# Two of eight column-block pairs of each SwiGLU input product in seven block products, with single plain columns between their half steps

## The chip, the core and the metric

One core of a Trainium2 chip runs the whole program. The metric is the device time of one execution in microseconds, the median of three runs. TensorE (PE in the profile) multiplies and writes to eight PSUM banks of 128 x 512 float32; VectorE (DVE) and ScalarE (ACT) empty the banks and prepare operands; SyncE (SP) issues the DMAs of the weights.

## The reference

Two layers on 256 tokens of width 2048. Each layer has three sublayers, each followed by a residual and a layer norm:

```python
x = layer_norm(ALPHA * x + 0.5 * swiglu(x, *ffn1[i]), *ln1[i])
x = layer_norm(ALPHA * x + mixers[i](x), *ln2[i])
x = layer_norm(ALPHA * x + 0.5 * swiglu(x, *ffn2[i]), *ln3[i])

def swiglu(x, w_in, w_out):
    a, gate = jnp.split(x @ w_in, 2, axis=-1)
    return (jax.nn.silu(a) * gate) @ w_out
```

The four `w_in` are 2048 x 8192 and the four `w_out` 4096 x 2048, all float32. The mixers are stick-breaking attention (layer 0) and causal window pooling (layer 1). The change touches only how `x @ w_in` and `silu(a) * gate` are computed, in all four SwiGLUs.

## The kernel before, in words

Activations lie with the features on the partitions and the 256 tokens beside them. Every float32 operand is split into two float32r parts, hi and lo, and a product is the sum of hi*hi, lo*hi and hi*lo. The tiles `xs` hold the parts of x, sixteen tiles of 128 features.

A weight block of 512 columns comes in chunks of 512 rows (1 MB, one DMA into `raw`, three buffers). `chunk` makes the parts of each chunk in two halves: ACT writes `whi` (L133), DVE subtracts it from `raw` and writes `wlo` (L134), with five buffers of each. `gemm` then multiplies: for each 128 x 128 piece of weights as the stationary operand, one product of 512 columns with the hi and lo parts of x side by side (L157) and one of 256 columns with the lo weights (L160). Four banks `ps` collect four tiles of 128 features, and the last chunk finishes one tile after the other, so that `total` (L194 on ACT, L195 on DVE) empties a bank while the others are still written.

`ffn_in` runs eight pairs of column blocks, one of `a` and one of the gate. Where a layer norm comes just before, the first pairs are multiplied with x that is not yet normed (`ahead`, L151 to L153, three products of 258 columns instead of 512 + 256), and the norm's result is applied to `xq` and `xs` in the hooks of the last of them (`apply`, L266 and after). One pair goes that way in most sublayers, two in the second SwiGLU of layer 0 (`npairs=2`). The gated tiles `g` are split into parts and multiplied with `w_out` in `sublayer_end`; the last sublayer does that with tokens as the stationary operand and 512 weight columns moving (L572 to L574), as `values` of the attention does (L428 to L430).

The Tile scheduler sets the order of each engine's instructions when the program is built; on the chip each engine goes through its list in order and waits on semaphores.

Of the kernel before, what the change touches and what calls it, by code (L numbers as in the profile page):

```python
# [13 lines left out]
P = 128  # L14
# [8 lines left out]
WINDOWS = (2, 4, 8, 16)  # L23
ALPHA = 4 ** 0.25
# [11 lines left out]
def trunk(ctx: ExitStack, tc: tile.TileContext, a: dict, out: bass.AP):  # L36
# [4 lines left out]
    whis = ctx.enter_context(tc.tile_pool(name="whis", bufs=5))  # L41
    wlos = ctx.enter_context(tc.tile_pool(name="wlos", bufs=5))
# [24 lines left out]
    # The tensor engine runs at its full clock only after a while of work: products for  # L67
    # nothing, until the first data is here.
# [7 lines left out]
    # tri[k', k] = 1 where k' >= k; past[k, q] = 1 where k < q, twice.  # L76
# [20 lines left out]

    def split(dst, hi_src, lo_src):
# [18 lines left out]
    def chunk(w, r, c, fine=False, step=4):  # L117
        """Four 128-row tiles of 512 columns of w, in halves of hi and lo parts."""
# [87 lines left out]
    class Norm:  # L206
        """LN of what x holds, less a shift: its statistics, 1 / std and -mean on all partitions,
        and its result, for four tiles at a time. Ahead of it, xs = [hi | lo] of gain * x."""
# [12 lines left out]
        def add(self, t):  # L221
            """Tiles t and t + 1."""
# [5 lines left out]
            else:  # L228
                sq = tmp.tile([P, 2 * T], F32, tag="sq", name="sq")
# [3 lines left out]
            gx = tmp.tile([P, 2, T], F32, tag="gx", name="gx")  # L233
# [4 lines left out]
        def stats(self):  # L238
            # Sums over the features, by token: means, then mean squares.
# [31 lines left out]
    def sublayer_end(w, rhs, factor, gname, bname, hooks=None, one=0):  # L271
        """x <- LN(ALPHA x + factor y): LN of x + (factor / ALPHA) y, with eps / ALPHA**2."""
# [43 lines left out]
    def ffn_in(w_in, norm, hooks=None, npairs=1):  # L316
        gs = [None] * (FF // P)
        for grp in range(FF // 512):
            acts = []
            nm = norm if grp < npairs else None  # L320

            def evac_a(f, ps, acts=acts, nm=nm):
                s = tmp.tile([P, T], F32, tag=f"act{f}", bufs=1, name="act")
# [304 lines left out]
```

## Time and profile before

| | |
|---|---|
| three runs | 2683.4, 2683.8, 2683.8 us; median 2683.8 us |
| span of the profiled execution | 2681.8 us; the median run is 2.0 us longer |
| busy: PE, DVE, ACT | 2666.7 us (99%), 1675.7 us (62%), 1365.4 us (51%) |
| granted TensorE clock | 0.998 of full speed over the span |
| DMA | 499.61 MB, mean 186 GB/s |

PE is busy nearly without a gap. A matmul's busy time in the rows is longer than its slot, since one begins before the one ahead of it has ended; the slot is the distance of two starts. In the same way DVE's instructions overlap a little at their ends. Only instructions that the profile shows are counted as busy.

### The profile page before, as it was taken

The numbers are of one execution on the slowest core, as the hardware profiler recorded it, in microseconds if no ns is written. First come the engines' busy times: TensorE is split into PE (matmuls) and PEld (weight loads), VectorE is DVE, ScalarE is ACT, GpSimd is POOL, SyncE is SP. The second block draws the span as 40 slices with busy tenths as digits, with TensorE's granted clock in tenths as the row PEclk, the third lists the DMA queues.
The fourth block names the chain that finished last, engine by engine and source line by source line (L and its number), as shares of the span: only waits on it lengthen the run. The fifth ranks groups of instructions, "written<-read, shape, count | busy, mean of one in ns | idle before, by whom it ended". The sixth has DMA issues, their size and how long they took to land.

```text
span 2681.8 us, 38727 instructions
## 1 busy us (share of the span) xinstructions
PE 2666.7 (99%) x15916; PEld 2365.1 (88%) x15916; DVE 1675.7 (62%) x2298; ACT 1365.4 (51%) x1990; POOL 11.9 (0%) x28
## 2 busy tenths in 40 slices
PE   9999999999999999999999999999999999999998
PEld 8888888899999888888988888889888998888886
DVE  6555556585686555565765555667878775555545
ACT  5444444467565444444654444445555565444432
POOL 0000000000000000000000000000000000000000
PEclk9999999999999999999999999999999999999999
DMA  7555555554455555555555555554555545555653
GB/s 255 188 188 187 189 188 189 189 174 162 153 190 183 187 186 186 199 177 201 173 189 189 189 189 189 189 189 170 192 189 176 201 174 182 186 186 187 228 193 126
DMA packets 71521, 499.61 MB, mean 186 GB/s; under 512 B 7984, under 2 KB 8624, under 8 KB 12080
## 3 DMA queue, kind: packets, MB, share of 16 engines
q1 hardware_dynamic: 70704, 495.05, 52.4%
q8 instruction: 124, 2.03, 0.3%
q0 software_dynamic: 640, 2.10, 0.2%
q14 instruction: 53, 0.43, 0.0%
HBM read 495.02 MB, written 2.10 MB: 185 GB/s over the span
## 4 chain that ended last, share of the span: by engine, by line
PE 99%; DVE 1%; DMA 0%; SPq 0%; ACT 0%; issue 0%; DVEq 0%; ACTq 0%
PE ps L157 50%; PE ps L160 26%; PE ps L152 5%; PE ps L151 5%; PE ps L153 5%; PE y L573 2%; PE y L572 2%; PE y L574 2%; PE v L430 1%; PE v L428 1%; PE v L429 1%; DMA xq<-in_x 0%; PE cum L407 0%; DVE z L547 0%; PE bc L257 0%; PE st L244 0%
## 5 line engine op out<-in xcount | busy, mean ns | idle before, releaser
L134 DVE TENSOR_TENSOR wlo<-raw,whi 128x1024 fp32r<-128x1024 f32 (+1 forms) x946 | 1144.3, 1212 | 905.8 <-ACT whi L133 901.2
L133 ACT CAST whi<-raw 128x1024 fp32r<-128x1024 f32 (+1 forms) x946 | 982.0, 1041 | 1080.1 <-PE ps L157 851.9
L157 PE MATMUL ps<-xs,whi 128*128 128x512 f32 x3968 | 1389.8, 396 | 1.1 <-ACT whi L133 0.7
L160 PE MATMUL ps<-xs,wlo 128*128 128x256 f32 x3968 | 1100.5, 280 | 1.0 <-DVE wlo L134 1.0
L157 PEld LDWEIGHTS ps<-xs,whi 128*128 128x128 f32 x3968 | 744.8, 189 | 173.4 <-ACT whi L133 1.0
L160 PEld LDWEIGHTS ps<-xs,wlo 128*128 128x128 f32 x3968 | 748.3, 189 | 7.3 <-DVE wlo L134 1.5
L157 PE MATMUL ps<-g,whi 128*128 128x512 f32 x1536 | 534.9, 394 | 0.0
L160 PE MATMUL ps<-g,wlo 128*128 128x256 f32 x1536 | 427.8, 280 | 0.0
L157 PEld LDWEIGHTS ps<-g,whi 128*128 128x128 f32 x1536 | 287.2, 187 | 65.3
L160 PEld LDWEIGHTS ps<-g,wlo 128*128 128x128 f32 x1536 | 289.7, 189 | 1.1
L152 PE MATMUL ps<-xs,whi 128*128 128x258 f32 (+1 forms) x896 | 252.7, 284 | 0.0
L151 PE MATMUL ps<-xs,whi 128*128 128x258 f32 (+1 forms) x896 | 251.7, 283 | 0.0
L153 PE MATMUL ps<-xs,wlo 128*128 128x258 f32 (+1 forms) x896 | 245.5, 282 | 0.0
L152 PEld LDWEIGHTS ps<-xs,whi 128*128 128x128 f32 x896 | 169.6, 189 | 0.2
L151 PEld LDWEIGHTS ps<-xs,whi 128*128 128x128 f32 x896 | 168.9, 188 | 0.0
L153 PEld LDWEIGHTS ps<-xs,wlo 128*128 128x128 f32 x896 | 167.6, 190 | 0.0
L194 ACT COPY half<-ps 128x256 f32<-128x256 f32 x264 | 97.1, 369 | 121.0 <-PE ps L157 119.6
L572 PE MATMUL y<-wlo,g 128*128 128x512 f32 x256 | 99.6, 389 | 0.0
L573 PE MATMUL y<-whi,g 128*128 128x512 f32 x256 | 99.6, 389 | 0.0
L574 PE MATMUL y<-whi,g 128*128 128x512 f32 x256 | 99.4, 389 | 0.0
L157 PE MATMUL ps<-y,whi 128*128 128x512 f32 x256 | 89.6, 396 | 0.0
L195 DVE TENSOR_TENSOR act<-ps,half 128x256 f32<-128x256 f32 x124 | 52.1, 421 | 46.6 <-ACT half L194 46.6
(151 smaller groups left out, 1677.0 us busy)
## 6 DMA issues: line engine op xcount, KB each, us to landing
raw<-in_l_ffn_w_in SPq DMA_DIRECT2D x252, 1024.0 KB, 4.8
raw<-in_l_ffn_w_out SPq DMA_DIRECT2D x127, 1024.0 KB, 4.8
raw<-in_l_pool_w_in SPq DMA_DIRECT2D x32, 1024.0 KB, 4.9
raw<-in_l_sb_w_qkv SPq DMA_DIRECT2D x24, 1024.0 KB, 4.8
raw<-in_l_pool_w_out SPq DMA_DIRECT2D x16, 1024.0 KB, 4.9
raw<-in_l_sb_w_o SPq DMA_DIRECT2D x8, 1024.0 KB, 4.9
raw<-in_l_pool_w_grp SPq DMA_DIRECT2D x4, 1024.0 KB, 4.9
raw<-in_l_ffn_w_in SPq DMA_DIRECT2D x6, 512.0 KB, 9.4
```

Of the source, the lines that this page charges most:

```text
L133: nc.scalar.copy(hi[:, i], src)
L134: nc.vector.tensor_tensor(out=lo[:, i], in0=src, in1=hi[:, i].bitcast(F32), op=ALU.subtract)
L151: nc.tensor.matmul(ps[:, :one], hi[:, cs], x[:, 0, :one], start=first, stop=False)
L152: nc.tensor.matmul(ps[:, :one], hi[:, cs], x[:, 1, :one], start=False, stop=False)
L153: nc.tensor.matmul(ps[:, :one], lo[:, cs], x[:, 0, :one], start=False, stop=last)
L157: nc.tensor.matmul(ps.rearrange("p (h n) -> p h n", h=2), hi[:, cs], x, start=first, stop=last)
L160: nc.tensor.matmul(ps[:, :T], lo[:, cs], x[:, 0], start=False, stop=False)
L194: nc.scalar.copy(t, ps[:, T:])
L195: nc.vector.tensor_tensor(out=dst, in0=ps[:, :T], in1=t, op=ALU.add)
L572: nc.tensor.matmul(ps[m], gh, lo, start=kk == 0, stop=False)
L573: nc.tensor.matmul(ps[m], gl, hi, start=False, stop=False)
L574: nc.tensor.matmul(ps[m], gh, hi, start=False, stop=kk == nk - 1)
```

## The change

In each SwiGLU the eight column-block pairs are now made in three ways.

- The first pair goes through `gemm` or `ahead` as before (`npairs=2` is gone).
- The last two pairs (`SEVENS = 2`) go through `Seven.run`. It takes the 256 x 2048 by 2048 x 1024 product as a 2 x 2 block product (tokens, features and columns halved) and does seven block products of 128 tokens x 1024 features x 512 columns instead of eight. Eight steps of 128 features each load 1 MB with the four weight blocks; DVE forms four sums of them (`ta`, `tb`, L400); all seven operands are split into parts; seven banks p1 to p7 collect the products, three matmuls of 512 columns a step each (L422 to L424), with the tokens as the stationary operand. `prepare` makes the sums of x and their parts, sixteen instructions of 128 x 512 on DVE and eight on ACT in each SwiGLU. At the end DVE adds the seven banks up, and after the gating PE transposes the tiles (eight transposes a pair) back to features on the partitions.
- The five pairs between are cut into 40 units of 128 columns (`column`): one DMA of 1 MB, two halves of parts, 16 x (512 + 256) matmul columns into one bank, which ACT copies out. Four go ahead of the seven products, one after each half step of them, and three at the end.

The gated tiles are kept whole in float32 and split later (`settle`). There are six buffers of `whi` and `wlo` instead of five, and two of the sums. The diff, cut to its core:

```diff
+SEVENS = 2
...
-    whis = ctx.enter_context(tc.tile_pool(name="whis", bufs=5))
-    wlos = ctx.enter_context(tc.tile_pool(name="wlos", bufs=5))
+    sums = ctx.enter_context(tc.tile_pool(name="sums", bufs=2))
+    whis = ctx.enter_context(tc.tile_pool(name="whis", bufs=6))
+    wlos = ctx.enter_context(tc.tile_pool(name="wlos", bufs=6))
...
+    def column(w, t):
+
+        raw = raws.tile([P, KT, P], F32, tag="raw", name="raw")
+        nc.sync.dma_start(raw, w[t])
...
+        ps = bank("pc")
+        for k in range(KT):
...
+                nc.tensor.matmul(ps.rearrange("p (h n) -> p h n", h=2), his[k], whole[k], start=k == 0,
+                                 stop=k == KT - 1)
...
+                nc.tensor.matmul(ps[:, :T], los[k], whole[k][:, 0], start=False, stop=False)
...
+        c = wide("col")
+        nc.scalar.copy(c, ps)
+        return c
...
+        def prepare(self, q):
+
+            a11, a21 = (xq[q][:, :, m * P:(m + 1) * P] for m in range(2))
+            a12, a22 = (xq[q + 2][:, :, m * P:(m + 1) * P] for m in range(2))
+            t = [wide(f"s{i}").rearrange("p (j n) -> p j n", j=4) for i in range(4)]
+            for dst, x, y, op in ((t[0], a21, a22, ALU.add), (t[1], t[0], a11, ALU.subtract),
+                                  (t[3], a12, t[1], ALU.subtract), (t[2], a21, a11, ALU.subtract)):
+                nc.vector.tensor_tensor(out=dst, in0=x, in1=y, op=op)
+            for i in (0, 1, 3, 2):
+                hi, lo = (scratch(16 + 8 * q + 2 * i + h, F32R, f"s{i}{q}{h}").rearrange("p (j n) -> p j n", j=4)
+                          for h in range(2))
+                nc.scalar.copy(hi, t[i])
+                nc.vector.tensor_tensor(out=lo, in0=t[i], in1=hi.bitcast(F32), op=ALU.subtract)
+                for j in range(4):
+                    self.s[i, 4 * q + j] = hi[:, j], lo[:, j]
...
+        def run(self, w, grp, between):
...
+                raw = raws.tile([P, 4, 512], F32, tag="raw", name="raw")
+                nc.sync.dma_start(raw, w[grp, i])
+                b11, b2, b22, b21 = raw[:, 1], raw[:, 2:4], raw[:, 3], raw[:, 2]
...
+                ta, tb = (sums.tile([P, 2, 512], F32, tag="sum", name=n) for n in ("ta", "tb"))
...
+                parts(h11, l11, b11)
+                hb, lb = pair()
+                parts(hb, lb, b2)
+
+                for dst, x, y in ((ta, raw[:, 0:1].to_broadcast([P, 2, 512]), raw[:, 1:4:2]),
+                                  (tb[:, 0], b22, ta[:, 0]), (tb[:, 1], b21, tb[:, 0])):
+                    nc.vector.tensor_tensor(out=dst, in0=x, in1=y, op=ALU.subtract)
+                ha, la = pair()
+                parts(ha, la, ta)
+                ht, lt = pair()
+                parts(ht, lt, tb)
...
+                x1, x2 = xs[i], xs[i + 8]
+                products = {
+                    1: ((x1[:, 0, :P], x1[:, 1, :P]), h11, l11),
+                    2: ((x2[:, 0, :P], x2[:, 1, :P]), hb[:, 0], lb[:, 0]),
+                    3: (self.s[3, i], hb[:, 1], lb[:, 1]),
+                    5: (self.s[0, i], ha[:, 0], la[:, 0]),
+                    7: (self.s[2, i], ha[:, 1], la[:, 1]),
+                    6: (self.s[1, i], ht[:, 0], lt[:, 0]),
+                    4: ((x2[:, 0, P:T], x2[:, 1, P:T]), ht[:, 1], lt[:, 1]),
+                }
+                order = (1, 2, 6, 5, 3, 7, 4) if i == 7 else tuple(products)
+                for h in range(2):
+                    for n in (order[:4] if h == 0 else order[4:]):
+                        (xh, xl), hi, lo = products[n]
+                        if i == 0:
+                            ps[n - 1] = bank(f"p{n}")
+                        p = ps[n - 1]
+                        nc.tensor.matmul(p, xh, hi, start=i == 0, stop=False)
+                        nc.tensor.matmul(p, xl, hi, start=False, stop=False)
+                        nc.tensor.matmul(p, xh, lo, start=False, stop=i == 7)
+                    if (i, h) != (7, 1):
+                        between(i, h)
...
+            nc.scalar.copy(s1, p1)
+            add(c11, p2, s1)
+            add(u2, p6, s1)
+            add(u4, p5, u2)
+            add(c12, p3, u4)
+            add(c22, p7, u4)
+            add(u2, p7, u2)
+            add(c21, p4, u2)
...
+        seven.prepare(0)
+        seven.prepare(1)
+        todo = list(range(4, 4 * (ng - SEVENS)))
...
+        early = len(units) - 16 * SEVENS
+        for _ in range(early // 2):
+            unit()
+        if hooks:
+            hooks()
...
+        def between(i, h):
+            unit()
+            if lates and (i, h) == (0, 1):
+                lates.pop()()
...
+        for grp in range(ng - SEVENS, ng):
+            acts, gates = seven.run(w_seven, grp - ng + SEVENS, between)
+            unit()
+            lates.append(gated(grp, silu(acts, acts), gates))
+        settle(range(8))
+        unit()
+        settle(range(8, 16))
+        lates.pop()()
+        while units:
+            unit()
+        settle(range(16, 32))
...
-    norm = ffn('l0_', 2, 'ln3', norm, npairs=2)
+    norm = ffn('l0_', 2, 'ln3', norm)
```

How the change moves the instructions, at two places. The first is PE in the first SwiGLU. Before, in a plain block, the last chunk goes from bank `ps0` to bank `ps1`, all four banks having been taken at the block's start (`xs` are the parts of x, `whi` and `wlo` those of the weights):

```order
L160 MATMUL ps0_779<-xs3_83,wlo_906 128x256
L157 MATMUL ps0_779<-xs3_83,whi_905 128x512
L160 MATMUL ps0_779<-xs3_83,wlo_906 128x256
L157 MATMUL ps0_779<-xs3_83,whi_905 128x512
L160 MATMUL ps1_780<-xs3_83,wlo_902 128x256
L157 MATMUL ps1_780<-xs3_83,whi_901 128x512
L160 MATMUL ps1_780<-xs3_83,wlo_902 128x256
```

Now, in the middle of the first run of seven products, a unit ends in bank `pc_1188`, the three matmuls of p1 follow, and the next unit begins in `pc_1269`:

```order
L341 MATMUL pc_1188<-xs3_86,whi_1184 128x512
L345 MATMUL pc_1188<-xs3_86,wlo_1185 128x256
L341 MATMUL pc_1188<-xs3_86,whi_1184 128x512
L422 MATMUL p1_828<-whi_1366,xs1_84 128x512
L423 MATMUL p1_828<-whi_1366,xs1_84 128x512
L424 MATMUL p1_828<-wlo_1367,xs1_84 128x512
L341 MATMUL pc_1269<-xs0_83,whi_1261 128x512
L345 MATMUL pc_1269<-xs0_83,wlo_1262 128x256 x2
L341 MATMUL pc_1269<-xs0_83,whi_1261 128x512
```

Seven of the eight banks hold p1 to p7 there, and both `pc` tiles lie in the one that is left; between the two units PE has three matmuls of 512 columns.

The second place is DVE in the second SwiGLU of layer 0, where the layer norm has just been applied and the first pair ends. Before, DVE empties the banks of the first gate block (`gate`) and makes the lo parts of the next chunks:

```order
L134 TENSOR_TENSOR wlo_7533<-raw_7530,whi_7532 128x1024
L134 TENSOR_TENSOR wlo_7537<-raw_7530,whi_7536 128x1024
L134 TENSOR_TENSOR wlo_7595<-raw_7592,whi_7594 128x1024
L189 SCALAR_TENSOR_TENSOR gate_7459<-rb_7174,aux_7460,ps0_7268 128x256
L189 SCALAR_TENSOR_TENSOR gate_7480<-rb_7174,aux_7481,ps1_7269 128x256
L191 TENSOR_TENSOR gate_7459<-gate_7459,rb_7174 128x256
L191 TENSOR_TENSOR gate_7480<-gate_7480,rb_7174 128x256
L336 SCALAR_TENSOR_TENSOR gate_7459<-gate_7459,aux_7460,act_7198 128x256
L336 SCALAR_TENSOR_TENSOR gate_7480<-gate_7480,aux_7481,act_7216 128x256
L134 TENSOR_TENSOR wlo_7599<-raw_7592,whi_7598 128x1024
```

Now the sums for the seven products (`s0`, `s1`, ... by `prepare`, their lo parts as `s001`, `s011`, ...) and the first steps' operands stand among them, up to the parts of the unit after the first half step (`wlo_7864`):

```order
L198 TENSOR_TENSOR gate_7549<-gate_7549,rb_7193 128x256
L198 TENSOR_TENSOR gate_7567<-gate_7567,rb_7193 128x256
L367 TENSOR_TENSOR s1_7610<-s0_7609,xq1_80 128x512
L372 TENSOR_TENSOR s011_7618<-s0_7609,s010_7617 128x512
L506 SCALAR_TENSOR_TENSOR gw1_7548<-gate_7549,aux_7550,act_7252 128x256
L506 SCALAR_TENSOR_TENSOR gw1_7548<-gate_7567,aux_7568,act_7252 128x256
L325 TENSOR_TENSOR wlo_7842<-tb_7825,whi_7841 128x1024
L367 TENSOR_TENSOR s3_7612<-xq3_82,s1_7610 128x512
L367 TENSOR_TENSOR s2_7611<-xq1_80 128x512
L325 TENSOR_TENSOR wlo_7864<-raw_7861,whi_7863 128x1024
```

DVE's list has gained the sums of x, the sums of the weights and the larger number of parts in this stretch; the chunks of plain blocks that stood here are gone from it.

## Rows read from the trace of the kernel before

**Rows 1.** The page: the span, and part 1, busy us of each engine

```profile
span 2681.8 us, 38727 instructions
...
PE 2666.7 (99%) x15916; PEld 2365.1 (88%) x15916; DVE 1675.7 (62%) x2298; ACT 1365.4 (51%) x1990; POOL 11.9 (0%) x28
```

**Rows 2.** Waits of PE: us in total, times, longest us

```profile
PE idle L71 <- DVE one_t L73: 1.1, 1, 1.1
...
PE ps L157 <- DVE gate L195: 0.5, 1, 0.5
```

**Rows 3.** Timeline of PE, plain block: start us, us, operation, idle before

```profile
2399.82 0.28 PE L160 MATMUL ps<-xs,wlo 128*128 128x256 f32 x1
...
2405.45 0.28 PE L160 MATMUL ps<-xs,wlo 128*128 128x256 f32 x1
```

**Rows 4.** Timeline, `values`: 512 weight columns moving, tokens stationary

```profile
670.71 0.40 PE L428 MATMUL v<-wlo,xs 128*128 128x512 f32 x1
...
673.50 0.39 PE L428 MATMUL v<-wlo,xs 128*128 128x512 f32 x1
```

**Rows 5.** Timeline of PE, `w_out` of the last sublayer, same form

```profile
2519.72 0.39 PE L573 MATMUL y<-whi,g 128*128 128x512 f32 x1
...
2523.80 0.39 PE L573 MATMUL y<-whi,g 128*128 128x512 f32 x1
```

**Rows 6.** Timeline of PE, `ahead`: three products of 258 columns

```profile
1292.31 0.29 PE L152 MATMUL ps<-xs,whi 128*128 128x258 f32 x1
...
1298.45 0.28 PE L152 MATMUL ps<-xs,whi 128*128 128x258 f32 x1
```

**Rows 7.** Timeline of PE, transposes of the last sublayer

```profile
2228.24 1.91 PE L524 MATMUL xt<-ident,xq 128*128 128x128 f32 x16
2229.91 0.36 PE L160 MATMUL ps<-xs,wlo 128*128 128x256 f32 x1
```

**Rows 8.** Timeline, pooling: a product that waits for its bank

```profile
1909.17 0.65 ACT L194 COPY half<-ps 128x256 f32<-128x256 f32 x2 [0.53 <-PE ps L157]
1909.82 0.75 DVE L195 TENSOR_TENSOR gate<-ps,half 128x256 f32<-128x256 f32 x2
...
1910.29 0.50 PE L157 MATMUL ps<-xs,whi 128*128 128x512 f32 x1 [0.45 <-DVE gate L195]
```

**Rows 9.** Timeline, layer 1: a bank of 512 columns copied by ACT

```profile
1310.42 1.05 PE L257 MATMUL bc<-ident,rn 128*128 128x128 f32 x8
...
1311.51 0.59 ACT L260 COPY rb<-bc 128x512 f32<-128x512 f32 x1
```

**Rows 10.** Groups by line and shape: count, busy us, mean ns, idle us

```profile
L134 DVE TENSOR_TENSOR wlo<-raw,whi 128x1024 fp32r<-128x1024 f32 x926 | 1131.2, 1223 | 898.9 <-ACT whi L133 894.6
...
L133 ACT CAST whi<-raw 128x1024 fp32r<-128x1024 f32 x926 | 970.4, 1050 | 1071.9 <-PE ps L157 851.9 <-PE y L574 93.8 <-PE ps L152 91.8
```

**Rows 11.** Timeline of DVE where a layer norm is applied

```profile
1312.77 4.90 DVE L266 TENSOR_TENSOR xq<-xq,rb 128x512 f32<-128x512 f32 x8
...
1324.71 1.22 DVE L134 TENSOR_TENSOR wlo<-raw,whi 128x1024 fp32r<-128x1024 f32 x1
1325.85 0.47 DVE L189 SCALAR_TENSOR_TENSOR act<-rb,aux,ps 128x256 f32<-128x256 f32 x1
1326.24 0.75 DVE L191 TENSOR_TENSOR act<-act,rb 128x256 f32<-128x256 f32 x2
1326.91 1.21 DVE L134 TENSOR_TENSOR wlo<-raw,whi 128x1024 fp32r<-128x1024 f32 x1
```

**Rows 12.** Busy us in two stretches: layer norm applied, and plain blocks

```profile
1317.00:1340.40 23.40, 23.40 (x196) 23.40 (x195) 22.46 (x37) 21.48 (x42) 0.00 (x0) 1.00 0.51 173
...
1400.00:1500.00 100.00, 100.00 (x572) 87.25 (x571) 56.31 (x72) 50.58 (x76) 0.00 (x0) 1.00 0.51 180
```

**Rows 13.** The page, part 3, last line: traffic of HBM

```profile
HBM read 495.02 MB, written 2.10 MB: 185 GB/s over the span
```

More of the change, by code (lines that the diff above doesn't have):

```diff
@@ L228, in add @@
             else:
[L229 removed]
+                sq = wide("sq")
                 nc.scalar.activation(sq, x, AF.Square)
@@ L313, in ahead, with parts @@
             gemm(w, col, xs, evac, hooks=hooks, one=W)
-    def ffn_in(w_in, norm, hooks=None, npairs=1):
-        gs = [None] * (FF // P)
[L318 to L323, printed above, removed]
+    def parts(hi, lo, src):
+        nc.scalar.copy(hi, src)
+        nc.vector.tensor_tensor(out=lo, in0=src, in1=hi.bitcast(F32), op=ALU.subtract)
@@ new lines, in ffn_in, with whole_pair, settle, silu @@
+    def ffn_in(w_in, w_columns, w_seven, norm, hooks=None):
+        ng = FF // 512
+        g32 = [None] * (FF // P // 2)
+        gs = [None] * (FF // P)
+        seven = Seven()
+        def whole_pair(i):
+            g32[i] = scratch(i, F32, f"gw{i}")
+            return g32[i]
+        def settle(ts):
+            for t in ts:
+                slot = 16 + t if t < 16 else 32 if t == 31 else t - 16
+                gs[t] = scratch(slot, F32R, f"g{t}").rearrange("p (h n) -> p h n", h=2)
+                src = g32[t // 2][:, t % 2 * T:(t % 2 + 1) * T]
+                split(gs[t], src, src)
+        def silu(a, src):
+            for m in range(2):
+                nc.scalar.activation(a[m], src[m], AF.Silu)
+            return a
+        def gated(grp, a, g):
+            for m in range(2):
+                nc.vector.tensor_tensor(out=a[m], in0=a[m], in1=g[m], op=ALU.mult)
+            def go():
+                for h in range(2):
+                    ps = bank("gt")
+                    for j in range(2):
+                        f = 2 * h + j
+                        for m in range(2):
+                            nc.tensor.transpose(ps[:, j * T + m * P:j * T + (m + 1) * P], a[m][:, f * P:(f + 1) * P],
+                                                ident)
+                    nc.scalar.copy(whole_pair(2 * grp + h), ps)
+            return go
+        def by_feature(grp):
+            acts, pairs = [], []
+            nm = norm
+            def evac_a(f, ps):
+                if f % 2 == 0:
+                    pairs.append(wide("act"))
+                s = pairs[-1][:, f % 2 * T:(f % 2 + 1) * T]
@@ L333, in evac_gate @@
                 if bias is None:
-                    nc.vector.tensor_tensor(out=g, in0=g, in1=acts[f], op=ALU.mult)
+                    nc.vector.tensor_tensor(out=dst, in0=g, in1=acts[f], op=ALU.mult)
                 else:
-                    nc.vector.scalar_tensor_tensor(out=g, in0=g, scalar=bias, in1=acts[f], op0=ALU.add, op1=ALU.mult)
-                split(gs[t], g, g)
-            ca, cg = (w_in, grp, evac_a), (w_in, FF // 512 + grp, evac_gate)
-            if nm is not None:
-                ahead(nm, (ca, cg), first=grp == 0, last=grp == npairs - 1)
-            else:
-                gemm(*ca[:2], whole, ca[2], hooks=(hooks or {}).get(grp), load=grp == 0 and norm is None)
-                gemm(*cg[:2], whole, cg[2])
@@ L345, in ffn_in @@
-        return gs
-    def ffn(p, i, ln, norm, npairs=1):
-        gs = ffn_in(a[f'{p}ffn{i}_w_in'], norm, npairs=npairs)
+                    nc.vector.scalar_tensor_tensor(out=dst, in0=g, scalar=bias, in1=acts[f], op0=ALU.add, op1=ALU.mult)
+            return (w_in, 0, evac_a), (w_in, 1, evac_gate)
+        ca, cg = by_feature(0)
+        if norm is not None:
+            ahead(norm, (ca, cg))
+        else:
+            gemm(*ca[:2], whole, ca[2], load=True)
+            gemm(*cg[:2], whole, cg[2])
@@ new lines, in ffn_in, with feature, half, first @@
+        seven.prepare(0)
+        seven.prepare(1)
+        todo = list(range(4, 4 * (ng - SEVENS)))
+        def feature(t):
+            def half(i):
+                c = column(w_columns, 2 * (t - 4) + i)
+                nc.vector.tensor_tensor(out=c[:, :T], in0=c[:, :T], in1=c[:, T:], op=ALU.add)
+                return c[:, :T]
+            def first():
+                s = half(0)
+                nc.scalar.activation(s, s, AF.Silu)
+                return s
+            def second(s):
+                g = half(1)
+                pair = whole_pair(t // 2) if t % 2 == 0 else g32[t // 2]
+                nc.vector.tensor_tensor(out=pair[:, t % 2 * T:(t % 2 + 1) * T], in0=g, in1=s, op=ALU.mult)
+            return first, second
@@ L481, in evac @@
             def evac(f, ps):
-                s = tmp.tile([P, T], F32, tag=f"act{f}", bufs=1, name="act")
+                if f % 2 == 0:
+                    pairs[:] = [wide("act")]
+                s = pairs[0][:, f % 2 * T:(f % 2 + 1) * T]
                 bias = total(s, ps, nm)
```

73 lines of the change are left out of this document (64 added, 9 removed).

## The prediction

> **What bounds the kernel now.** I read the page first. PE is busy 2666.7 of 2681.8 us, DVE 62%, ACT 51% [rows 1]. PE's waits come next: the longest is 1.1 us at the start, and the only one on a bank is 0.5 us [rows 2]. So the time is the sum of PE's slots, and a change pays if it takes slots away and PE still never waits. The timeline of PE gives the slots, as distances of starts. In a plain block sixteen pairs of 256 and 512 columns take 2405.45 - 2399.82 = 5.63 us, 0.352 us a pair [rows 3]. Where tokens are stationary and 512 weight columns move, which is the form of the seven products, twelve matmuls take 2.79 us, 0.2325 each [rows 4]; in the last sublayer eighteen take 4.08 us, 0.2267 each [rows 5]. Three of 258 columns in `ahead` take 6.14 / 17 = 0.361 us [rows 6].
>
> **PE's slots.** A pair of column blocks was 2 x 16 x 4 = 128 pairs of matmuls; the seven products are 7 x 8 x 3 = 168 matmuls of 512 columns. Two pairs in each of four SwiGLUs make eight: 1024 x 0.352 = 360.4 us go, 1344 x 0.2325 = 312.5 us come, -47.9 us. I take 0.2325 because `values` has the same stationary `xs` and runs in the midst of the layer, as the products will. At 0.2267 it is 304.7, so -55.7; at 0.24, which I set as far above as 0.2267 lies below and a little more, 322.6, so -37.8.
>
> The Trainium skill ("TensorE: Matmul & The Clock Gate", Back-to-back issue gap) gives N / 2.4 + 2.5 ns at full clock, 215.8 ns for 512 columns and 109.2 for 256; by it the change would be 1344 x 0.2158 - 1024 x 0.3250 = -42.8 us. The rows differ, 0.2325 or 0.2267 against 0.2158, and the measurement decides.
>
> The second pair of `npairs=2` becomes plain: 128 x (0.361 - 0.352) = -1.2 us. The 40 units keep the 16 x 0.352 us of the same columns. Eight transposes for each of the eight pairs are new: 64 at 1.67 / 16 = 0.104 us [rows 7], +6.7 us. PE's sum is -47.9 - 1.2 + 6.7 = -42.4 us.
>
> **What DVE and ACT get.** A step of the seven products makes 3.5 tiles of parts instead of the two of a plain chunk, and four sums; two units stand beside it. Without their overlapping ends DVE's instructions take 1.14 us for 1024 columns (1324.71 to 1325.85), 0.60 for 512 (eight in 4.90), 0.39 with a scalar operand and 0.335 for 256 [rows 11]. A step on DVE is then seven lo parts and `ta`, 8 x 1.14, three of 512 (half a tile of parts, two sums), 1.8, and three of 256 from the units, 1.0: 11.9 us. On PE it is 21 x 0.2325 + 32 x 0.352 = 16.1 us. DVE is 74% full, where plain blocks fill it to 56% [rows 12]; ACT's share, eight casts of at most 1.05 us [rows 10], two copies of 0.59 [rows 9] and a Silu, is 10 us. Both are hidden by PE as long as their work arrives in time. The DMA of a step is 3 MB in 16.1 us against the present 185 GB/s [rows 13], within 6%, and the packets keep their 8 KB; I cost it at nothing. The `settle` splits are the splits of before at another place, under the last units; nothing.
>
> **Waits that come.** First the bank. Seven products hold seven banks and every unit uses the eighth. After a unit's last matmul starts, 0.40 us to its end [rows 4], same shape, 0.04 until ACT begins (1310.42 + 1.05 to 1311.51), 0.59 for the copy [rows 9], and 0.05 until PE has the bank (DVE's first gate ends at 1909.82 + 0.42, PE starts at 1910.29 [rows 8]): 1.08 us, 0.85 more than the matmul's slot. What PE does in between covers it. In the order eight places in each SwiGLU have less than 1.3 us between two uses of one bank: three with three matmuls of 512 (0.70 us, 0.15 left), two with two (0.46, 0.39 left), three with four or more (nothing left). 3 x 0.15 + 2 x 0.39 = 1.2 us, times four +4.9 us. I take the copy as first in ACT's line there: the cast ahead of it gets its buffer in the middle of the unit, 2.8 us before. Nor below zero: a wait can't give time back. If each copy stood behind a full cast of 1.05 us it would be 8.9 us a SwiGLU, 35.7.
>
> Second, the front of the SwiGLU. While a norm is applied DVE is busy 22.46 of 23.40 us already [rows 12], and now `prepare` follows. It is worst in the second SwiGLU of layer 0. From its first evacuation, 2.5 us before the gate block starts, to `wlo_7864` DVE has 40 instructions of 512, 17 of 1024, 10 with a scalar, 8 of 256: 24.0 + 19.4 + 3.9 + 2.7 = 50 us, ready at 47.5. PE wants it after 64 x 0.361 + 64 x 0.352 + 15 x 0.2325 = 49.1 us. Between them are 1.6 us; queued behind that instruction are all parts of the next step, and PE waits for them. With DVE idle 4% as in that stretch, 2 us, it is 0.4 late, and a little more in the step after: I take +2 us. With the full durations (1.22 for 1024 and so on) it would be about 56, 4.4 late; if all three normed SwiGLUs were as late, 13 us. In the other two the prepared rows stand later, so I stay near the low end.
>
> Third, the changes of runs: eight runs hand seven banks over by DVE's seven additions, under a unit of 5.6 us. No row shows it; between 0 and one turnaround of 1.08 us each, I take 0.4, +3 us.
>
> **Sum.** 2681.8 - 42.4 + 4.9 + 2 + 3 = 2649.3 us of span. The median run is 2.0 us above the span, so 2651 us. The bounds together: -55.7 - 1.2 + 6.7 = -50.2 with no wait gives 2634; -37.8 + 5.5 + 4.9 + 13 + 8.6 = -5.8 gives 2678.
>
> **Rivals.** A: no new wait shows and a slot is 0.2267, as in the last sublayer. For it: PE waits nowhere now. Against it: one bank for all units. 2634 us.
>
> B: the bank is the bound of the stage: the copy stands behind casts, and 35.7 us of waits come with the 2 + 3 above. For it: ACT has one list and 10 us of casts and copies in 16. Against it: the gaps between casts in the present lists. 2681.8 - 42.4 + 40.7 + 2.0 = 2682 us. The Trainium skill speaks for this one ("Perfetto Trace Analysis", Optimizing Tensor Performance): independent groups of matmuls should rotate through PSUM banks, so that one is emptied under the next one's matmuls. By that rule the units lose here; no row of before shows such a stage, the nearest being the 0.5 us of rows 2.
>
> C, on the other side: the tile pairs run out. Six pairs are filled by the half tile, a unit's two and a step's three, so the parts of a sum can be begun only when PE has passed the first half of a unit. They are due 2.8 + 1.4 us later, and a cast and a subtraction take 1.05 + 1.22 = 2.27 [rows 10]: 1.9 us are to spare. If lists of ACT and DVE come late by that, the chain is laid bare once in two steps: 32 x 2.27 = 72.6 us, 2681.8 - 32.5 + 72.6 + 2.0 = 2724 us. It decides from 32.5 / 32 = 1.0 us in two steps. For it: DVE stands idle 894.6 us for ACT's casts now [rows 10], so the two work in lockstep. Against it: DVE has a quarter of each step free.
>
> **Chances.** Forecast 0.60 (its own range 2634 to 2678), A 0.07, B 0.20, C 0.13. The range that leaves out no more than 2 in 10 is 2634 to 2682. A difference below 0.2%, 5.4 us, can't be told from none. The forecast and A are faster; of B, which ends near 2682, half lies below 2678 and half within 0.2%; C is slower. Faster 0.77, same 0.10, slower 0.13.
>
> **What would show it.** Right: on PE 448 more matmuls of 512 columns, 896 fewer of 256 and 384 fewer of 258 (1344 - 1024 + 128, 1024 - 128, 3 x 128), those of p1 to p7 0.2325 us apart, PE waits of 0.1 to 0.4 us on the copy of `pc` at five places a SwiGLU, a few us in all ahead of the first `pc` unit after the first half step, DVE near 74% in the runs. Wrong: waits of a microsecond on `pc` (B), or on `whi` and `wlo` inside the runs in every second step (C); a slot of 0.24 or more, or a granted clock that falls below 1.00 after such waits, would take the gain as well.

## The result, and the profile after

The changed kernel takes 2653.9 us (median of four runs, 2653.9 to 2654.3), the kernel before, beside it on the same chip, 2683.8 us: a ratio of 0.9889 (95% interval 0.9875 to 0.9903), 29.9 us faster. The forecast was 2651 us and a range of 2634 to 2682.

The page of the changed kernel, which answers to [rows 1] and [rows 13]:

```profile
span 2652.2 us, 37769 instructions
...
PE 2632.2 (99%) x15148; PEld 2303.4 (87%) x15148; DVE 1964.3 (74%) x2650; ACT 1476.5 (56%) x2094; POOL 11.9 (0%) x28
...
HBM read 495.02 MB, written 2.10 MB: 187 GB/s over the span
```

PE is as full as before and the span is 29.6 us shorter: PE has less to do. DVE has 289 us more and still is not the bound. The waits of PE (us in total, times, longest):

```profile
PE pc L341 <- ACT col L350: 2.9, 6, 1.3
...
PE idle L75 <- DVE one_t L77: 1.1, 1, 1.1
...
PE pc L341 <- ACT gw L483: 0.8, 4, 0.2
PE p L422 <- ACT whi L324: 0.5, 1, 0.5
```

Against [rows 2], new are waits on the copy that empties a unit's bank (`col<-pc`, L350) and a few more at the same place; the longest is 1.3 us. There is none on `whi` or `wlo` in every second step. The timeline of PE in a run, products with `xs` and with `s`, and a unit up to the next product (start us, us, operation):

```profile
102.09 0.40 PE L422 MATMUL p<-whi,xs 128*128 128x512 f32 x1
...
104.63 0.39 PE L422 MATMUL p<-whi,s 128*128 128x512 f32 x1
...
105.54 0.39 PE L341 MATMUL pc<-xs,whi 128*128 128x512 f32 x1
...
111.17 0.40 PE L422 MATMUL p<-whi,s 128*128 128x512 f32 x1
```

Eleven matmuls of the products take 104.63 - 102.09 = 2.54 us, 0.231 each, a little less than `values` in [rows 4]; sixteen pairs of a unit 5.63 us, 0.352, as in [rows 3].

To see where the time went I summed the distances from each start on PE to the next, by the output of the first of the two, so that a wait counts for the matmul before it. "Late" is what distances more than 25 ns above their usual slot have too much.

| output, us | before | after | of it late |
|---|---|---|---|
| `ps` (plain blocks, `ahead`, `w_out`) | 2415.4 | 1154.5 | 6.3, after 4.5 |
| `pc` (units) | | 905.5 | 3.9 |
| `p` (seven products) | | 319.4 | 9.1 |
| `gt` (transposes) | | 5.7 | |

The difference of these sums, -30.3 us, is the change of the span but for 0.7 us: the transposes of the last sublayer (`xt`), which now stand just ahead of the last SwiGLU's runs, take 1.5 us more, the start-up and the end 0.9 less.

### The profile page after: what moved, and what is told of

It is laid out like the page before. It is cut to its first block, busy times and chain, and to the rows that moved or that the text cites. A ratio compares the mean times of both kernels' runs of the same rounds, so it can differ in the third digit from the quotient of the medians.

```text
span 2652.2 us, 37769 instructions
## 1 busy us (share of the span) xinstructions
PE 2632.2 (99%) x15148; PEld 2303.4 (87%) x15148; DVE 1964.3 (74%) x2650; ACT 1476.5 (56%) x2094; POOL 11.9 (0%) x28
## 4 chain that ended last, share of the span: by engine, by line
PE 98%; ACT 1%; DVE 0%; DMA 0%; SPq 0%; issue 0%; DVEq 0%; ACTq 0%
PE pc L341 23%; PE ps L164 21%; PE pc L345 12%; PE ps L167 10%; PE ps L159 4%; PE ps L158 4%; PE ps L160 4%; PE p L422 4%; PE p L423 4%; PE p L424 4%; PE y L805 2%; PE y L806 2%; PE y L804 2%; PE v L660 1%; PE v L658 1%; PE v L659 1%
## 5 line engine op out<-in xcount | busy, mean ns | idle before, releaser
L341 PE MATMUL pc<-xs,whi 128*128 128x512 f32 x2560 | 914.5, 397 | 3.7 <-ACT col L350 2.9
L345 PE MATMUL pc<-xs,wlo 128*128 128x256 f32 x2560 | 694.0, 281 | 0.0
L341 PEld LDWEIGHTS pc<-xs,whi 128*128 128x128 f32 x2560 | 481.6, 189 | 116.8 <-ACT col L350 10.4
L325 DVE TENSOR_TENSOR wlo<-raw,whi 128x1024 fp32r<-128x1024 f32 (+1 forms) x448 | 503.0, 1144 | 47.4 <-ACT whi L324 28.9
L345 PEld LDWEIGHTS pc<-xs,wlo 128*128 128x128 f32 x2560 | 483.7, 189 | 13.0
L350 ACT COPY col<-pc 128x512 f32<-128x512 f32 x160 | 93.9, 588 | 224.0 <-PE pc L341 222.0
L159 PE MATMUL ps<-xs,whi 128*128 128x258 f32 (+1 forms) x768 | 218.3, 284 | 0.0
L158 PE MATMUL ps<-xs,whi 128*128 128x258 f32 (+1 forms) x768 | 217.6, 283 | 0.0
L164 PE MATMUL ps<-xs,whi 128*128 128x512 f32 x512 | 178.9, 396 | 0.9 <-ACT whi L140 0.9
L160 PEld LDWEIGHTS ps<-xs,wlo 128*128 128x128 f32 x768 | 146.2, 190 | 0.0
L159 PEld LDWEIGHTS ps<-xs,whi 128*128 128x128 f32 x768 | 145.4, 189 | 0.2
L158 PEld LDWEIGHTS ps<-xs,whi 128*128 128x128 f32 x768 | 144.6, 188 | 0.0
L167 PE MATMUL ps<-xs,wlo 128*128 128x256 f32 x512 | 141.0, 281 | 1.6 <-DVE wlo L141 1.6
```

The source lines that it names most:

```text
L158: nc.tensor.matmul(ps[:, :one], hi[:, cs], x[:, 0, :one], start=first, stop=False)
L159: nc.tensor.matmul(ps[:, :one], hi[:, cs], x[:, 1, :one], start=False, stop=False)
L160: nc.tensor.matmul(ps[:, :one], lo[:, cs], x[:, 0, :one], start=False, stop=last)
L164: nc.tensor.matmul(ps.rearrange("p (h n) -> p h n", h=2), hi[:, cs], x, start=first, stop=last)
L167: nc.tensor.matmul(ps[:, :T], lo[:, cs], x[:, 0], start=False, stop=False)
L325: nc.vector.tensor_tensor(out=lo, in0=src, in1=hi.bitcast(F32), op=ALU.subtract)
```

## The experiments

The diffs are against the changed kernel where nothing else is said, and cut to what matters. Times are medians; ratios are to the kernel before, with their 95% interval.

**Is a step of seven hidden only by its units?** The units are taken out of the runs:

```diff
+        for _ in range(16 * SEVENS):
+            unit()
...
-            unit()
             if lates and (i, h) == (0, 1):
```

> All 32 units of a SwiGLU that stood behind half steps now run ahead of its two runs; the seven products follow one another with nothing between them. My theory (a step of seven costs DVE more than PE and lives on the units' cover): DVE needs 4 x 1.14 + 3 x 0.60 = 6.4 us a step, PE 21 x 0.232 = 4.9; over the 16 steps of a SwiGLU 16 x 6.4 - 16 x 4.9 = 24 us come bare, less the lead of six filled tile pairs, about 10 us: +15 us a SwiGLU, +60 in all, less the 7 us of waits on the one bank: 2653.9 + 53 = 2707 us (2690 to 2735), with PE waits on whi and wlo in every step of the runs and none on pc's bank. Rival (PE alone sets the time, the interleaving is worth nothing): 2653.9 - 7 = 2647 us, PE without waits in the runs.

Measured: 2796.3 us, ratio 1.0419 (1.0404 to 1.0435). The rival is out by 149 us, but my number was far too low. The runs of one SwiGLU, by busy time (span, sum with counts, then PE, PEld, DVE, ACT, POOL; the granted clock, DMA share, GB/s):

```profile
280.00:360.00 80.00, 64.41 (x237) 44.47 (x236) 79.61 (x100) 45.60 (x66) 0.00 (x0) 0.94 0.41 143
```

DVE is busy 79.61 of 80 us and PE only 64: DVE is the bound, as I said. I had left out the end of each run, seven sums and two gate products on DVE, 9 x 0.60 = 5.4 us (two expectations below count eight sums). With them 16 x 6.4 + 2 x 5.4 - 10 of lead is 103 us a SwiGLU against 78 on PE, 25 bare; the products' late time is 111.2 / 4 = 27.8. The units behind the runs are late too (35.8 us in all), and most of that is DVE again: the transpositions among them wait for its last gate products.

```profile
PE gt L481 <- DVE c L473: 24.1, 4, 6.7
```

Towards the end of the first of these four waits the clock fell, 0.75 in the slice from 370 to 380 us. With 24.1 / 4 = 6.0 a SwiGLU DVE's price is 34 us for the 25 of the mended sum; what makes the rest stays open.

**What does the one bank cost?** First, a second copy of it:

```diff
         nc.scalar.copy(c, ps)
+        nc.scalar.copy(c, ps)
```

> The copy that empties a unit's bank is made twice, one behind the other (0.59 us more on ACT for each of 160 units). The order is planned anew by it: no two uses of the one bank then stand within 1.08 us, against 24 places before. With two copies the turnaround is 1.67 us. My theory (the bank costs only where too few matmuls stand between two units): the 5 us of bank waits and some 2 us behind them go or shrink to the four places at 1.39 us (0.3 each): 2653.9 - 5 = 2649 us (2645 to 2654). Rival (the copy's place in ACT's list sets the step, case B of the prediction): each longer copy is felt, 128 x 0.59 = 75 us, or at the least at the 24 places, 14 us: 2668 to 2729 us.

Measured: 2709.8 us, 1.0099 (1.0084 to 1.0114): 55.9 us slower than the changed kernel, inside the rival's range. My theory failed, though the bank was the smaller part of it. The waits (L351 is the second copy, and what follows it in the kernel stands one line further on):

```profile
PE p L423 <- ACT whi L324: 30.2, 48, 1.8
PE pc L341 <- ACT col L351: 12.8, 26, 0.9
```

Of these two, more than two thirds are on a cast. One of the 48, in the timeline:

```profile
131.44 0.40 PE L423 MATMUL p<-whi,xs 128*128 128x512 f32 x1
131.65 0.59 ACT L350 COPY col<-pc 128x512 f32<-128x512 f32 x1 [2.20 <-PE pc L341]
...
132.13 1.05 ACT L324 CAST whi<-raw 128x1024 fp32r<-128x1024 f32 x1
133.07 0.59 ACT L351 COPY col<-pc 128x512 f32<-128x512 f32 x1
...
133.23 0.50 PE L423 MATMUL p<-whi,xs 128*128 128x512 f32 x1 [0.93 <-ACT whi L324]
```

To keep units apart, the scheduler now puts two or more products behind this unit. The second needs a cast that stands in ACT's list behind the unit's copy: the copy begins when the unit ends, the cast when the copy ends, and the first product's three matmuls cover 0.7 of the 133.23 - 131.44 = 1.8 us. That is case C, a cast laid bare, and not in every second step by a late DVE but by where the unit stands. The changed kernel has the same cast behind the same copy, but there a unit follows the first product and hides it, and PE pays for the bank. The timeline of that place:

```profile
128.43 0.39 PE L341 MATMUL pc<-xs,whi 128*128 128x512 f32 x1
...
128.86 0.59 ACT L350 COPY col<-pc 128x512 f32<-128x512 f32 x1 [2.20 <-PE pc L341]
...
129.12 0.39 PE L424 MATMUL p<-wlo,xs 128*128 128x512 f32 x1
129.34 1.05 ACT L324 CAST whi<-raw 128x1024 fp32r<-128x1024 f32 x1
...
129.49 0.50 PE L341 MATMUL pc<-xs,whi 128*128 128x512 f32 x1
```

From 129.12 to 129.49 are 0.37 us, 0.14 more than a slot. What part of the 56 us the order has and what the longer copy could not be told apart, since the order could not be held with two copies; in the place shown the second copy stands behind the cast, and it is not what PE waits for.

A shorter copy does keep the order nearly as it was. It leaves out the right half of a unit's result:

```diff
-        nc.scalar.copy(c, ps)
+        nc.scalar.copy(c[:, :T], ps[:, :T])
...
-                nc.vector.tensor_tensor(out=c[:, :T], in0=c[:, :T], in1=c[:, T:], op=ALU.add)
+                nc.vector.tensor_tensor(out=c[:, :T], in0=c[:, :T], in1=c[:, :T], op=ALU.add)
```

> Only the left 256 columns of a unit's bank are copied, and the sum takes that half twice (the right half of the unit's result is left out); the order on PE stays as in the changed kernel but for a few places, with the units behind three matmuls of a product where they stood. My theory (a unit waits there for the copy of the unit before, 0.14 us with a copy of 0.59): an ACT instruction of 256 columns takes 0.42, so 0.17 less; the places with three matmuls between lose their wait, the longer ones half of it, and the 0.1 us behind each goes with it: 2653.9 - 4 = 2650 us (2648 to 2652.5). Rival (these 0.14 us are the hand-over between two uses of a bank, whatever the copy takes): the waits stay, 2653.9 us within 1.

Measured: 2652.3 us (2651.8 to 2654.8), 0.9885 (0.9868 to 0.9901); the time does not tell the two apart. The trace does. The same place:

```profile
129.61 0.39 PE L341 MATMUL pc<-xs,whi 128*128 128x512 f32 x1
...
130.04 0.37 ACT L350 COPY col<-pc 128x256 f32<-128x256 f32 x1 [2.20 <-PE pc L341]
...
130.30 0.44 PE L424 MATMUL p<-wlo,xs 128*128 128x512 f32 x1
...
130.58 0.40 PE L341 MATMUL pc<-xs,whi 128*128 128x512 f32 x1
```

The copy takes 0.37 instead of 0.59, and the distance falls from 0.37 to 0.28. Where two matmuls stand between, the excess falls from 0.37 to 0.16; at the place behind a transpose, whose bank another copy empties, it stays at 0.37. So the wait is the copy, and it is worth a few us.

**Are the tile pairs what a step hangs on?**

```diff
-    whis = ctx.enter_context(tc.tile_pool(name="whis", bufs=6))
-    wlos = ctx.enter_context(tc.tile_pool(name="wlos", bufs=6))
+    whis = ctx.enter_context(tc.tile_pool(name="whis", bufs=5))
+    wlos = ctx.enter_context(tc.tile_pool(name="wlos", bufs=5))
```

> Five filled hi and lo tile pairs instead of six. My theory (the chain of cast and subtraction has more than a tile of room): no wait on whi or wlo in the runs; by the places in the order of PE where one bank is used twice within 1.08 us, bank waits of 8.4 us instead of 5.4: 2653.9 + 3 = 2657 us (2652 to 2664). Rival (the tile pairs are what the step hangs on, case C of the prediction): one cast and one subtraction, 2.27 us, laid bare once in one or two steps: +73 to +145 us, 2727 us or more, PE waiting on whi or wlo in the runs.

Measured: 2657.2 us, 0.9903 (0.9886 to 0.9919), the number of my theory, but not its waits. No wait on `whi` or `wlo` of a run appears; new is

```profile
PE gt L481 <- ACT col L350: 2.8, 4, 0.8
```

a transposition that waits for the units' bank. Late time is 2.9 us less in `p`, 3.0 more in `pc`, and the transpositions take 1.8 more; behind the longest wait of a unit, 1.78 us at the front of the second SwiGLU, the granted clock was 0.52 from 817.0 to 820.4 us, which I had not counted. With the number of pairs the order changes as well, so this shows that five can be enough, not that a pair is never missed.

**How does the time go with the number of pairs?** One by seven:

```diff
-SEVENS = 2
+SEVENS = 1
```

> One column-block pair of a SwiGLU by seven, 48 units, one behind each half step of the one run, 16 ahead. My theory (the gain is a sum of slots for each pair, its waits for each run): relative to the changed kernel 512 x 0.3522 = 180.3 us more of units, 672 x 0.2309 = 155.2 and 32 x 0.09 = 2.9 less, and about half of the 13 us of waits less: 2653.9 + 22.2 - 6 = 2670 us (2666 to 2674). Rival (most of the cost is fixed for a SwiGLU and not for a run: prepare, the front, the tail): with the same waits as with two runs, 2676 us, and the second pair would be worth more than the first.

Measured: 2664.2 us, 0.9928 (0.9912 to 0.9944). Both theories miss: the first pair gives 19.6 us, the second 10.3. In the trace the one run is nearly free of waits (late: 2.1 us in `p`, 1.5 in `pc`, against 9.1 and 3.9 with two). It starts behind sixteen units instead of four, so that the front is past, and no transposes fall into it.

Three by seven, with one unit behind a whole step:

```diff
-SEVENS = 2
+SEVENS = 3
...
-        early = len(units) - 16 * SEVENS
+        early = len(units) - 8 * SEVENS
...
-            unit()
+            if h == 1:
+                unit()
```

> Three column-block pairs of a SwiGLU by seven products, and 32 units, one behind each whole step instead of each half step. My theory (PE's slots set the time as long as a step's DVE work is below PE's): 512 pairs of the units' matmuls go, 512 x 0.3533 = 180.9 us; 672 x 0.232 = 155.9 us and 32 transposes, 3.3 us, come; the order has no two uses of the one bank within 1.08 us, so some 6 us of waits go: 2653.9 - 28 = 2626 us (2618 to 2640). DVE has 4 x 1.14 + 3 x 0.60 + 2.6 = 9.0 us a step of 10.5 on PE, 85%. Rival (half the cover makes DVE and its chain late): 2.27 us laid bare once in two steps, 48 x 2.27 = 109 us: 2653.9 - 28 + 109 = 2735 us, with PE waits on whi and wlo in the runs.

Measured: 2652.3 us, 0.9884 (0.9869 to 0.9898); neither. The slots are as forecast, but `p` is late by 28.9 us. The place, on DVE, at the change from the first run to the second:

```profile
154.38 1.22 DVE L325 TENSOR_TENSOR wlo<-raw,whi 128x1024 fp32r<-128x1024 f32 x1
155.51 0.69 DVE L434 TENSOR_TENSOR u<-p,su 128x512 f32<-128x512 f32 x1
...
168.85 0.70 DVE L473 TENSOR_TENSOR c<-c,c 128x512 f32<-128x512 f32 x1
170.19 1.23 DVE L400 TENSOR_TENSOR ta<-raw 128x1024 f32<-128x1024 f32 x1 [0.65 <-DMA raw<-in_l_ffn_w_in_seven]
```

and what PE then waits for:

```profile
168.40 0.73 PE L424 MATMUL p<-wlo,s 128*128 128x512 f32 x2 [0.40 <-DVE wlo L325]
170.15 0.50 PE L422 MATMUL p<-whi,s 128*128 128x512 f32 x1 [1.02 <-ACT whi L324]
...
172.61 0.51 PE L424 MATMUL p<-wlo,s 128*128 128x512 f32 x1 [1.26 <-DVE wlo L325]
```

While PE has two whole steps, 44 matmuls, in a row with no unit between, DVE works without a gap from the first sum to the last gate product. After that product DVE stands idle 0.65 us for the weights of a step, which is part of the last of these waits. So I put a unit there (the diff is against three_by_seven):

```diff
-        early = len(units) - 8 * SEVENS
-        for _ in range(early // 2):
+        for _ in range(3):
...
-            if h == 1:
+            if h == 1 or i == 0:
                 unit()
```

> Three column-block pairs by seven, as in three_by_seven, but the first step of each run has a unit behind both halves, and one unit less stands ahead of the runs and two less behind them. In the order of three_by_seven 44 and 36 matmuls of the products stood in a row at the changes of runs, and its waits on whi and wlo (28.9 us late in the products' slots, against 9.1 in the changed kernel) stand there. My theory (at the change DVE has eight sums and two gate products more, some 6 us, in which PE needs the cover of a unit): most of that goes, 28.9 to about 10: 2652.3 - 18 = 2634 us (2628 to 2645). Rival (DVE is simply full at one unit a step, wherever the units stand): the waits move to other steps and the time stays at 2652 us (2648 to 2660).

Measured: 2637.6 us, 0.9827 (0.9814 to 0.9841). Late in `p` are 10.2 us. The units and products are the same; three of 32 units, placed otherwise, are worth 14.7 us.

Four by seven, five units to a run:

```diff
-SEVENS = 2
+SEVENS = 4
...
-        early = len(units) - 16 * SEVENS
-        for _ in range(early // 2):
+        for _ in range(3):
...
-            unit()
+            if h == 1 and i % 2 == 0:
+                unit()
```

> Four column-block pairs by seven and 24 units: three ahead, five to each run (behind the steps 1, 3, 5, 7 and the run), one behind. My theory (a step of products is worth it only as far as its DVE work is covered): against three_eased PE's slots give 512 x 0.3522 = 180.3 less and 155.4 + 2.9 more, -22 us; but DVE in the four runs of a SwiGLU has 32 x 6.4 + 4 x 6.0 + 20 x 2.6 = 281 us and PE 32 x 4.85 + 20 x 5.64 = 268: some 13 us a SwiGLU come bare, 52 in all: 2637.6 - 22 + 52 = 2668 us (2640 to 2700), with PE waits on whi and wlo throughout the runs. Rival (DVE catches up under the units): 2616 us.

Measured: 2728.7 us, 1.0165 (1.0151 to 1.0179), slower than the kernel before. The direction holds, the size does not. Two slices of 10 us in the first SwiGLU:

```profile
140.00:150.00 10.00, 6.60 (x25) 4.03 (x24) 10.00 (x14) 3.62 (x4) 0.00 (x0) 0.98 0.46 171
150.00:160.00 10.00, 9.83 (x32) 7.53 (x33) 10.00 (x15) 6.57 (x9) 0.00 (x0) 0.68 0.44 143
```

DVE is full in both. In the first PE was busy 6.6 us of ten; in the second it is busy again, at a mean granted clock of 0.68, so for most of the slice at the lower of its two levels, 1.2 GHz. My 13 us a SwiGLU were DVE's 281 us over PE's 268, as if DVE never stood idle. From the first to the last product the four SwiGLUs take 285.3, 302.6, 299.0 and 291.1 us, 26.5 more than 268 in the mean, with DVE busy 283.6 and idle 10.9. One thing that keeps a list from going on is the weights, on which ACT waits 66.7 us here and 5.9 in the changed kernel:

```profile
ACT whi L324 <- DMA raw<-in_l_ffn_w_in_seven: 66.7, 50, 3.3
```

More buffers of `raw` were not tried. What the low clock costs is not told apart either, since DVE is full while it is low.

**The front.** Six units ahead and two behind, instead of four and four:

```diff
-        for _ in range(early // 2):
+        for _ in range(3 * early // 4):
```

> Six units ahead of the runs instead of four, and two behind them instead of four. My theory (the waits at 814 and 1349 us, 1.8 us each, are DVE's list of the applied norm, the prepared sums and the first parts being late): two units more give DVE 11 us, and these waits go: 2653.9 - 3.5 = 2650.4 us (2648.5 to 2653). Rival (the wait moves with the first units, or the two units are missed at the end, where the last gated tiles are split): 2654 to 2659 us.

Measured: 2651.8 us, 0.9881 (0.9867 to 0.9895). The interval overlaps that of the changed kernel; in the trace the waits at the front are gone, and the late time of `p` and `pc` is 3.5 us less, as my theory had it; that DVE's list made those waits is not shown (see below). But the plain blocks take 3.0 us more (`ps` 1157.5), 2.5 of them in slots of the blocks with `g`, 0.3504 us a pair for 0.3488, though nothing in them was changed; neither theory names this.

**The size of a slot.** Rows of `xs` 264 elements apart:

```diff
-    xsq = [res.tile([P, 4, 2, W], F32R, ...) for q in range(4)]
+    xsq = [res.tile([P, 4, 2, 264], F32R, ...)[:, :, :, :W] for q in range(4)]
...
```

> The rows of the tokens' parts in SBUF (xs) are 264 elements apart instead of 258, so that the 256 tokens of each start at a multiple of 32 bytes; a gate tile shares its buffers with another to make room. One theory (where TensorE reads rows that start off such a multiple, a slot is longer: pairs with xs take 0.3510 in plain blocks and 0.3522 in units, with g, whose rows are aligned, 0.3488; products with xs stationary 0.2335, with s 0.2297): 3072 pairs x 0.0024 + 576 x 0.0038 = 9.6 us go: 2644 us (2642 to 2648). Rival (the slots differ by the order of matmuls and banks): no change, 2653.9 us within 2.

Measured: 2649.7 us, 0.9872 (0.9858 to 0.9886). A matmul of a unit falls from 176.1 to 174.8 ns in the mean, 6.7 us in all, and a plain pair with `xs` from 0.3512 to 0.3501 us without late time: where the rows of `xs` move, units fall by what the theory took, 2.6 ns a pair for 2.4, and plain pairs by half of it. Products with `xs` stationary stay (0.2322 us in the changed kernel, 0.2321 here), where the theory took 3.8 ns, and those with `s`, whose rows were not touched, fall by 1.2 ns. Blocks with `g` take 2.5 us more, as in six_ahead, so that is not the layout, and `xt` 1.7 more. The layout counts, then, for the moving rows; that it does so by multiples of 32 bytes, one other distance does not show. The other reason, the order of banks:

```diff
             if c < n - 1:
-                for k in range(4):
-                    for f in range(4):
+                for f in range(4):
+                    for k in range(4):
```

> In the plain blocks the four pairs of a bank follow one another, so that a bank is written eight times in a row and the moving columns change with each pair, as they do in a unit; before, the banks took turns and four pairs in a row had the same moving columns. Theory (that is why a pair takes 0.3522 us in a unit and 0.3510 in a plain block with xs): the plain pairs with xs go to 0.3522, those with g from 0.3488 to about 0.350, +3 us. Rival (it is the form of the unit's weight tiles): the plain pairs stay, 2653.9 us.

One execution: 2663.2 us, 9.3 more than the changed kernel, where my theory had 3 and the rival none; 3.0 of that is late time in `p`. Pairs with `g` go from 0.3488 to 0.3520 us. But the last chunk of each of these blocks, which finishes one bank after the other in both kernels, goes from 0.3482 to 0.3513 as well, so the order of banks is not shown to be the cause. Pairs with `xs`, on which the theory rested, go from 0.3509 to 0.3513 where the order was changed, a third of the way. This run decides nothing, then; the rows of the kernel before tell more (in the next section).

**Together.** Three by seven, the eased changes of runs, the wider rows, four units ahead:

```diff
-SEVENS = 2
+SEVENS = 3
...
+    xsq = [res.tile([P, 4, 2, 264], F32R, ...)[:, :, :, :W] for q in range(4)]
...
+        for _ in range(4):
             unit()
...
+            if h == 1 or i == 0:
+                unit()
```

> three_eased with the rows of xs 264 elements apart and four units ahead of the runs and one behind instead of three and two. If the measured parts add up: units 4096 x 1.3 ns and products 2016 x 0.7 ns less, plain blocks 1.4 us more, as in rows_264, -5 us; of the waits at the front of the normed SwiGLUs (1.25 us at the start of the runs, and 3 us behind in the second SwiGLU) about 3 us less, as six_ahead had: 2637.6 - 8 = 2630 us (2626 to 2636). Rival (the order is planned anew and other waits come in their place): 2636 to 2645 us.

Measured: 2629.7 us (2626.7 to 2631.6), 0.9800 (0.9786 to 0.9813), 54.0 us below the kernel before as my sum had it, and the best of all. That it met the sum is in part luck: against three_eased late time of `p` and `pc` falls by 7.6 us instead of 3, and a wait of 2.8 us in `xt` that I had not counted takes some back.

## Why the prediction was right

**PE's slots** were right: the 1344 products took 310.3 us without their late time (0.2309 each, 0.2325 taken), the removed 1024 pairs about 0.351 x 1024 = 359.4, so -49.1 for -47.9. `npairs` gave -1.3 for -1.2, the transposes +5.7 for +6.7. PE's sum is -44.7 for -42.4. The counts came as forecast: 448 more matmuls of 512 columns, 896 and 384 fewer of 256 and 258.

**The step that failed in size** is "The 40 units keep the 16 x 0.352 us of the same columns". Without their waits units take 0.3522 us a pair; what they replaced took 0.3509 in the mean over all plain blocks with `xs`: 2560 x 0.0013 = +3.3 us. The sixteen pairs of [rows 3] are not such a mean. They are the last chunk of a block, which finishes one bank after the other, as a unit does; in the chunks before it the four banks take turns. Thirteen pairs of such a chunk, in the next block of the kernel before:

```profile
2407.32 0.40 PE L157 MATMUL ps<-xs,whi 128*128 128x512 f32 x1
...
2411.88 0.39 PE L157 MATMUL ps<-xs,whi 128*128 128x512 f32 x1
```

They take 4.56 us, 0.3508 a pair. Over the 62 plain blocks with `xs` of that trace a pair takes 0.3508 us in the first three chunks and 0.3519 in the last. So the rows I took were like a unit, and not like most of what went. Why a pair with `g` does not follow this (0.3488 and 0.3482) stays open.

**The bank**, +4.9, was right: at the five places of each SwiGLU the excess was 0.14 three times and 0.37 twice, 1.2 us, 4.7 in all. Another 0.25 stood ahead of the transposes, and 0.1 us behind each wait. One of the two longer places is behind a transpose, not behind a unit. The Trainium skill ("Perfetto Trace Analysis", Optimizing Tensor Performance) asks that independent groups of matmuls rotate through PSUM banks. Here 128 units shared one bank for these few us, because other banks' matmuls stood between; where they did not, the wait came, so the rule's reason agrees with the trace and its price was small, 8.3 us even with all of the front's 3.6.

**The front**, +2, was 3.6, not only where I looked and not by the wait that I forecast, so that its size came out near by luck. The timeline of PE in the second SwiGLU of layer 0 and in the first of layer 1:

```profile
813.68 0.39 PE L424 MATMUL p<-wlo,s 128*128 128x512 f32 x1
815.34 0.50 PE L341 MATMUL pc<-xs,whi 128*128 128x512 f32 x1 [1.26 <-ACT col L350]
...
1349.09 0.39 PE L424 MATMUL p<-wlo,s 128*128 128x512 f32 x1
1350.22 0.51 PE L341 MATMUL pc<-xs,whi 128*128 128x512 f32 x1 [0.75 <-ACT col L350]
1351.26 0.50 PE L422 MATMUL p<-whi,xs 128*128 128x512 f32 x1 [0.53 <-ACT whi L324]
```

The first place is the forecast one, the first unit behind the first half step. But PE waits there for the copy of the one bank, and not for DVE's parts (`wlo_7864`). ACT and DVE at that place:

```profile
811.37 1.05 ACT L324 CAST whi<-raw 128x1024 fp32r<-128x1024 f32 x1 [1.27 <-PE pc L341]
813.23 1.05 ACT L324 CAST whi<-raw 128x1024 fp32r<-128x1024 f32 x1 [0.81 <-PE p L423]
814.19 0.61 ACT L371 CAST s<-s 128x512 fp32r<-128x512 f32 x1
814.71 0.58 ACT L350 COPY col<-pc 128x512 f32<-128x512 f32 x1
...
812.92 3.48 DVE L325 TENSOR_TENSOR wlo<-raw,whi 128x1024 fp32r<-128x1024 f32 x3
```

The first of the three lo parts on DVE is the unit's and ends at 812.92 + 1.21 = 814.13; an undelayed PE, which has one matmul of the unit and two of the products ahead of it, would want it at 813.68 + 4 x 0.23 = 814.60. The bank's last matmul had ended at 811.3, but its copy stands behind two casts, the second of which waits for its buffer, and a cast of the prepared sums: B's order, at one place. At the second place it is the same, with the copy at 1349.60. I had stayed "near the low end" for the other normed SwiGLUs; the second place cost 1.8 us like the first.

**The changes of runs**, +3, cost nothing that shows: a unit hides the seven sums. Where it is not there the first change of a SwiGLU cost 3.2 us (three_by_seven, 0.57 + 1.19 + 1.42 above the slots). **DVE's share** in the runs is 79% instead of 74%:

```profile
90.00:210.00 120.00, 120.00 (x634) 102.23 (x633) 95.28 (x112) 66.91 (x84) 0.00 (x0) 1.00 0.54 187
```

95.28 of 120 us: a busy time counts the overlapping ends, 1.22 and not 1.14 for 1024 columns, which the step's sum did not.

So late time came to 13.0 us for 9.9 forecast, and the units' slot to 3.3 for none; the slots gave 2.3 more than forecast, and the plain blocks were late 1.8 less: -30.2 of the -30.3 summed above. The span of 2652.2 lies 2.9 us from the forecast 2649.3, nearer than the terms, because these errors partly cancel. **Rivals.** A is out: no slot of 0.2267, and waits came. B is out as the bound of the stage, but its order makes the front's two waits. C is out for this kernel, not for its neighbours: products that wait for a cast are most of the waits in copy_twice, 30.2 us, and DVE is full for most of the runs in units_apart and four_by_seven.

## What to carry to other kernels

Cutting TensorE's work pays only as far as VectorE's share of each stretch is covered, so add up that share between two fillers, the ends of the runs included, and put the filler where it is highest: moving three units of each SwiGLU was worth 14.7 us. A wait can be the price of cover elsewhere: in copy_twice the order that took two units apart, for a bank wait of 0.14 us, laid a cast of 1.05 us bare. A matmul's slot depends on its neighbours and on the layout by a per cent, so take it from as many rows as it will be multiplied by, and from rows in the same order.

## What the runs showed of the hardware

In four_by_seven the granted clock was 0.98 in a slice of ten us with PE busy for 6.60, 0.68 in the next and then 1.00 again; in five_pairs it was 0.52 from 817.0 to 820.4 us, just behind a wait of 1.78 us; in the changed kernel, whose longest wait is 1.3 us, it is 0.999 over the span. A pair of 512 and 256 columns took 0.3522 us in units; in plain blocks with `xs` 0.3508 with the banks in turn and 0.3519 with one bank after the other; with `g` 0.3488, 0.3504 (six_ahead, rows_264) or 0.3520 (bank_by_bank), where the step to 0.3504 came with nothing changed in those blocks. Rows of `xs` 264 elements apart took 2.6 ns off a pair in units and 1.1 in plain blocks. A PSUM copy on ACT took 0.37 us for 256 columns and 0.59 for 512.
